# A two-block transformer on one Trainium2 core: the mixer's probabilities scaled by ScalarE, and its q and k norms split into two steps

## The chip, the core and the metric

The kernel runs on one core of a Trainium2 chip. The metric is the device time of one execution in microseconds; three runs are given, with their median. A profile of one execution gives a span (first to last instruction) and, for every instruction, when it started and how long it took. The engines are TensorE (PE; its weight loads, PEld, are listed apart), VectorE (DVE), ScalarE (ACT), GpSimd (POOL) and the DMA queues, which SyncE (SP) issues here.

## The reference

512 tokens of 1024 channels, float32. The first block has two layers: differential attention (8 heads, two softmaxes a head, their difference normalised per head), a gated FFN with a 3-wide convolution, a gated embedding; then the same with windowed attention. The second block is what most of the change is in, the *mixer*:

```python
h = rmsnorm(x, g_mix); proj = h @ w_in
a_in, q, k, v, f_logit, gate_a, gate_b = split(proj)
y_conv = silu(layernorm(causal_depthwise_conv(glu(a_in), w_dw, b_dw))) @ w_conv_out   # 31 taps, 512 channels
q, k = rmsnorm per head (8 heads of 64)
s = q k^T / 8 + c[q] - c[k], causal        # c: running sum of log sigmoid(f_logit + b_forget)
y_attn = softmax(s) v @ w_attn_out
x = x + (sigmoid(gate_a) * y_conv + sigmoid(gate_b) * y_attn) @ w_out
```

followed by a second gated FFN. All of it must come out in float32.

## The kernel before

Each float32 operand is held as a high and a low part, and a product is three matmuls: high with high, high with low, low with high (lines 188, 189, 190, in `mm3`). Weights arrive by DMA as `wr`; `wh` is cast from them by ACT (line 157) and `wl` is subtracted by DVE or POOL (line 158). `split` (lines 180 to 184) makes the two parts of an activation: ACT writes the high part, DVE the low one. All 512 tokens are one tile of 128 channels by 512 columns (the free dimension), so a projection (`dense`) is 24 matmuls of 512 columns.

The stages follow one another: differential attention from about 60 to 330 us of the span, FFN, embedding, windowed attention, FFN, embedding, the mixer from about 1340 to 1665, the last FFN.

**The order of the work.** The program is written as generators that yield where other work may step in. A scheduler then puts every engine's instructions in an order of its own, by place in the program and by what is ready in its model, and each engine runs its list strictly in that order. Tiles come from pools of a few buffers per tag. PSUM has 2 banks of tag `acc` (projections), 3 of `sc` (scores `ps_s` and sums of squares `ps_ss`), 1 of `po` and 2 of `tp`; they are handed out in program order. In SBUF the tag `C` of pool `fp` has 3 buffers, which the norm's `isq`, `isl`, `dg`, `iy` and POOL's convolution product `tap` share.

**The norm.** `inv_rms` (line 406) is used by both attentions. It takes the bank `ps_ss` first; with `eps` given (differential attention) `row_mm` puts two matmuls with diagonals `dg` (lines 211, 217) into it. Then ACT squares (`isq`, line 413) and copies (`ish`, 416), POOL or DVE subtracts (`isl`, 417), two matmuls add (lines 418, 419), ACT takes logarithm, exponential and a square, and DVE does two steps (424, 425) to `iy`. `head_norm` of the differential attention calls it on each head's output (POOL subtracts, DVE for heads 5 and 6). In the mixer `unit_heads` (line 968) reads a projection, calls `inv_rms` without `eps`, multiplies (972) and splits into `qhl`; `qk(m)` does so for k, yields, for q, yields, and then copies both by DMA into the stacks `st` of a pair of heads.

**The mixer's attention.** `head` (line 1000 on) has four row tiles of 128, 256, 384 and 512 columns: scores into an `sc` bank, DVE adds the decay and takes the maximum (1021), ACT exponentiates and sums (1026, recorded as line 146), DVE inverts the sum (1027) and scales (1028), PE transposes (1036), `split` makes `ah` and `al`, three matmuls add to `ps_o`. The first start is `qk(0)`, `vproj(0)`, `glu(2)`, `glu(3)` one after another (1056); the loop over heads (1064 to 1075) then mixes in the other projections, and after each row tile a convolution tap for POOL: `tap` times a weight (921) into a `C` buffer, added to `cacc` (924).

Of the kernel before, what the change touches and what calls it, by code (L numbers as in the profile page):

```python
# [19 lines left out]
P = 128  # L20
# [71 lines left out]
def build(tc, nc, a, out):  # L92
# [313 lines left out]
    def inv_rms(u, sel, n, eps=None, eng=G):  # L406


        ps = att.tile([P, T], F32, tag="sc", name="ps_ss", bufs=BANKS["sc"])
        if eps is not None:  # L410
            row_mm(ps, eps, eng, False)
        sq = fp.tile([P, T], F32, tag="C", name="isq")
# [3 lines left out]
        S.copy(out=sh, in_=sq)  # L416
        eng.tensor_tensor(out=sl, in0=sq, in1=rd(sh), op=ALU.subtract)
        TE.matmul(ps, sel, sh, start=eps is None, stop=False)
        TE.matmul(ps, sel, sl, start=False, stop=True)
# [5 lines left out]
        V.scalar_tensor_tensor(out=y, in0=sq, scalar=-3.0 * n / 64, in1=y, op0=ALU.add, op1=ALU.mult)  # L425
        return y, inv_rms_factor(n)


    def diff_attention(nm, nxt):
# [77 lines left out]
        def head_norm(hd):  # L507

            o = of[hd]
            eps = sm.tile([P, 4], F32, tag="eps", name="eps", bufs=2)  # L510
            s0 = sums[hd][:, :, 0]
            V.scalar_tensor_tensor(out=eps, in0=s0, scalar=P * EPS, in1=s0, op0=ALU.mult, op1=ALU.mult)
            eng = V if hd in HNV else G
            w, _ = inv_rms(o, onesr, P, eps, eng)
            eng.tensor_tensor(out=o, in0=o, in1=w, op=ALU.mult)
# [342 lines left out]
    def mix(nm, nxt):  # L858
# [109 lines left out]
        def unit_heads(ps, g, tag, bufs):  # L968

            u = evac_scaled(ps, nm.rb)  # L970
            w, f = inv_rms(u, blkr, 64, None, V)
            V.tensor_tensor(out=u, in0=u, in1=w, op=ALU.mult)
# [3 lines left out]
            split(hl[:, 0], hl[:, 1], u, gs)  # L976
            return hl

        sts = {}

        def qk(m):

            pk = dense("w_qk2", 2 * m + 1, x)
            hk = unit_heads(pk, gqk[:, 1:2], "hk", 1)
            yield
            pq = dense("w_qk2", 2 * m, x)
            hq = unit_heads(pq, gqk[:, 0:1], "hq", 1)
            yield
            for j in range(2):
                sl = slice(64 * j, 64 * j + 64)  # L990
# [11 lines left out]
        def head(hd):  # L1002
# [7 lines left out]
            for i in range(4):  # L1010
# [16 lines left out]
                V.reciprocal(out=su, in_=su)  # L1027
                V.tensor_scalar(out=e[:, :wd], in0=e[:, :wd], scalar1=su, scalar2=None, op0=ALU.mult)
                ee.append(e)
# [25 lines left out]

        for _ in chain(qk(0), vproj(0), *(glu(m) for m in (2, 3))):
            pass
        for m in (2, 3):
# [277 lines left out]
```

## Time and profile before

| | |
|---|---|
| runs | 2095.48, 2098.79, 2099.24 us; median 2098.79 |
| profiled execution | 2097.09 us, its span 2095.3 us |
| mean granted TensorE clock | 0.983 of 2.4 GHz |
| PE busy | 2013.4 us, 96% of the span |
| DVE / ACT / POOL busy | 1378.0 / 899.4 / 454.7 us |

PE's share says that it is nearly always at work, so that an engine beside it matters only where PE stands still. Where that is, the windows and the waits tell. 1.8 us of the execution lie outside the span.

### The profile page before, as it was taken

Reading aid. Unit: us, or ns where it says so; the run is one execution under the profiler, and the core shown is the slowest. Engines: PE = TensorE matmul, PEld = TensorE weight load, DVE = VectorE, ACT = ScalarE, POOL = GpSimd, SP = SyncE. Lnnn points to the kernel's source line nnn. Section 1 sums busy time; section 2 is a strip of 40 time slices with the busy share of each in tenths; the row PEclk is TensorE's granted clock in tenths of the full one; section 3 lists DMA queues with packets and bytes.
Section 4 is the critical chain, followed back from the end, with each engine's and each line's share of the span. In section 5 each row is a group of like instructions: output and inputs, shape, how many; then the busy total and the mean of one; then the engine's idle time right before and its main releaser. Section 6 shows DMA issues by size and latency. Waiting matters only on the chain.

```text
span 2095.3 us, 25046 instructions
## 1 busy us (share of the span) xinstructions
PE 2013.4 (96%) x9374; PEld 1655.5 (79%) x9374; DVE 1378.0 (66%) x2189; ACT 899.4 (43%) x1431; POOL 454.7 (22%) x322
## 2 busy tenths in 40 slices
PE   7999889999999999889999999999999899999999
PEld 6888668888888877668888888778778688888887
DVE  7776858747466757777647466778889764434443
ACT  5565635424244435554424235446546343222221
POOL 2464322000002226310000001305599030000000
PEclk9999989999999999999999999999999999999999
DMA  4543422233233253112232323233322232232232
GB/s 164 167 121 105 147 71 91 82 109 101 92 100 132 100 171 111 41 41 91 90 110 92 101 94 115 94 108 112 88 86 71 81 101 96 96 101 96 95 101 91
DMA packets 69465, 212.43 MB, mean 101 GB/s; under 512 B 9568, under 2 KB 9568, under 8 KB 68832
## 3 DMA queue, kind: packets, MB, share of 16 engines
q1 hardware_dynamic: 69344, 210.84, 31.5%
q8 instruction: 74, 1.21, 0.2%
q14 instruction: 47, 0.39, 0.1%
HBM read 179.31 MB, written 6.29 MB: 89 GB/s over the span
## 4 chain that ended last, share of the span: by engine, by line
PE 80%; DVE 9%; POOL 5%; issue 2%; ACT 2%; DMA 2%; SPq 1%; DVEq 0%; POOLq 0%; ACTq 0%
PE ps_d L188 25%; PE ps_d L190 24%; PE ps_d L189 24%; POOL cacc L924 3%; POOL tap L921 1%; DVE wl L158 1%; PE ps_o L189 1%; PE ps_s L395 1%; PE ps_o L188 1%; PE ps_o L190 1%; PE ps_s L396 1%; DMA qst<-rt 1%; SPq L385 1%; PE ps_t L674 1%; DVE xq L184 1%
## 5 line engine op out<-in xcount | busy, mean ns | idle before, releaser
L157 ACT CAST wh<-wr 128x1024 fp32r<-128x1024 f32 (+1 forms) x323 | 338.0, 1048 | 659.0 <-PE ps_d L189 551.2
L188 PE MATMUL ps_d<-xO,wh 128*128 128x512 f32 x1400 | 547.2, 392 | 5.6 <-ACT wh L157 3.2
L190 PE MATMUL ps_d<-xO,wl 128*128 128x512 f32 (+1 forms) x1400 | 547.2, 391 | 0.8 <-DVE wl L158 0.8
L189 PE MATMUL ps_d<-xV,wh 128*128 128x512 f32 (+1 forms) x1400 | 546.4, 391 | 0.0
L158 DVE TENSOR_TENSOR wl<-wr,wh 128x1024 fp32r<-128x1024 f32 x286 | 367.3, 1286 | 90.3 <-ACT wh L157 87.9
L188 PEld LDWEIGHTS ps_d<-xO,wh 128*128 128x128 f32 x1400 | 262.8, 188 | 62.5 <-ACT wh L157 4.5
L190 PEld LDWEIGHTS ps_d<-xO,wl 128*128 128x128 f32 (+1 forms) x1400 | 262.7, 188 | 57.5 <-DVE wl L158 2.0
L189 PEld LDWEIGHTS ps_d<-xV,wh 128*128 128x128 f32 (+1 forms) x1400 | 262.9, 188 | 55.6 <-DVE xV L184 0.2
L271 POOL TENSOR_TENSOR ss<-ss,sq 128x512 f32<-128x512 f32 x44 | 69.4, 1577 | 815.4 <-ACT sq L269 801.9
L314 DVE TENSOR_TENSOR u<-ps_d,rb 128x512 f32<-128x512 f32 x156 | 106.3, 687 | 203.5 <-PE ps_d L190 196.4
L189 PE MATMUL ps_d<-gl,wh 128*128 128x512 f32 x528 | 204.3, 389 | 0.0
L188 PE MATMUL ps_d<-gh,wh 128*128 128x512 f32 x528 | 203.0, 389 | 0.0
L190 PE MATMUL ps_d<-gh,wl 128*128 128x512 f32 x528 | 203.0, 389 | 0.0
L188 PE MATMUL ps_d<-xq,wh 128*128 128x512 f32 x448 | 179.3, 404 | 21.8 <-ACT wh L157 10.1
L190 PE MATMUL ps_d<-xq,wl 128*128 128x512 f32 x448 | 179.4, 401 | 1.3 <-DVE wl L158 1.3
L189 PE MATMUL ps_d<-xq,wh 128*128 128x512 f32 x448 | 180.0, 402 | 0.4 <-DVE xq L184 0.4
L763 DVE TENSOR_TENSOR h<-h,ps_d 128x512 f32<-128x512 f32 x72 | 48.6, 685 | 176.7 <-PE ps_d L190 176.7
L188 PEld LDWEIGHTS ps_d<-xq,wh 128*128 128x128 f32 x448 | 86.7, 194 | 41.9 <-ACT wh L157 10.3
L188 PEld LDWEIGHTS ps_d<-gh,wh 128*128 128x128 f32 x528 | 99.1, 188 | 20.6
L190 PEld LDWEIGHTS ps_d<-gh,wl 128*128 128x128 f32 x528 | 99.1, 188 | 20.6
L189 PEld LDWEIGHTS ps_d<-gl,wh 128*128 128x128 f32 x528 | 99.1, 188 | 20.5
L158 POOL TENSOR_TENSOR wl<-wr,wh 128x1024 fp32r<-128x1024 f32 x37 | 90.5, 2449 | 109.0 <-ACT wh L157 94.3
(313 smaller groups left out, 3112.2 us busy)
## 6 DMA issues: line engine op xcount, KB each, us to landing
wr<-w_up SPq DMA_DIRECT2D x132, 512.0 KB, 3.4
wr<-w_dn SPq DMA_DIRECT2D x66, 512.0 KB, 3.5
wr<-w_qk SPq DMA_DIRECT2D x34, 512.0 KB, 3.5
qst<-rt SPq DMA_DIRECT2D x64, 128.0 KB, 2.7
wr<-w_pg SPq DMA_DIRECT2D x16, 512.0 KB, 3.5
wr<-w_g SPq DMA_DIRECT2D x16, 512.0 KB, 3.4
wr<-w_v SPq DMA_DIRECT2D x14, 512.0 KB, 3.5
st<-qhl SPq DMA_DIRECT2D x48, 128.0 KB, 2.3
```

Source lines behind the costliest of these rows:

```text
L157: S.copy(out=hi, in_=raw)
L158: lo_eng[0].tensor_tensor(out=lo, in0=raw, in1=rd(hi), op=ALU.subtract)
L184: V.scalar_tensor_tensor(out=lo, in0=src, scalar=scale, in1=rd(hi), op0=ALU.mult, op1=ALU.subtract)
L188: TE.matmul(ps, lh, rh, start=start, stop=False)
L189: TE.matmul(ps, lh, rl, start=False, stop=False)
L190: TE.matmul(ps, ll, rh, start=False, stop=stop)
L271: (V if self.first and k not in SSP else G).tensor_tensor(out=self.ss, in0=self.ss, in1=sq, op=ALU.add)
L314: V.tensor_tensor(out=u, in0=ps, in1=rb, op=ALU.mult)
L385: Q.dma_start(out=rd(t[64 * b : 64 * b + 64]), in_=rd(hl[32 * j : 32 * j + 32, 2 * z : 2 * z + 2]))
L395: TE.matmul(ps, q[:, qc], k[:, kc], start=True, stop=False)
L763: V.tensor_tensor(out=h[m], in0=h[m], in1=ps, op=ALU.add)
L924: G.tensor_tensor(out=accs[m], in0=accs[m], in1=t, op=ALU.add)
```

## The change

The scaling of the probabilities (line 1028 before, 1033 after) is written for ACT: a copy with the inverted sum as its scale. `inv_rms` becomes a generator with two steps: squares and their two parts; then, after a `yield`, the bank, the matmuls and the rest. `unit_heads` and `qk` pass the break on, so in the mixer the second step of the norm of k comes after another projection, and the second step of q's after one more. At the start the program's order is now k's projection and first step, v's projection, rest of k's norm with q's projection and first step, half of `glu(2)`, rest of q's norm with the stacks, and what is left of the glus. `head_norm` runs both steps at once, but in it the bank and the two `dg` matmuls now come behind `isq`, `ish` and `isl`.

```diff
--- before.py
+++ after.py
@@ -406,15 +406,16 @@
     def inv_rms(u, sel, n, eps=None, eng=G):
 
 
-        ps = att.tile([P, T], F32, tag="sc", name="ps_ss", bufs=BANKS["sc"])
-        if eps is not None:
-            row_mm(ps, eps, eng, False)
         sq = fp.tile([P, T], F32, tag="C", name="isq")
         S.activation(out=sq, in_=u, func=AF.Square)
         sh = fp.tile([P, T], F32R, tag="A", name="ish")
         sl = fp.tile([P, T], F32R, tag="C", name="isl")
         S.copy(out=sh, in_=sq)
         eng.tensor_tensor(out=sl, in0=sq, in1=rd(sh), op=ALU.subtract)
+        yield
+        ps = att.tile([P, T], F32, tag="sc", name="ps_ss", bufs=BANKS["sc"])
+        if eps is not None:
+            row_mm(ps, eps, eng, False)
         TE.matmul(ps, sel, sh, start=eps is None, stop=False)
         TE.matmul(ps, sel, sl, start=False, stop=True)
         y = fp.tile([P, T], F32, tag="C", name="iy")
@@ -423,7 +424,7 @@
         S.activation(out=sq, in_=y, func=AF.Square, scale=0.125)
         V.scalar_tensor_tensor(out=sq, in0=ps, scalar=epsn[n] if eps is None else 0.0, in1=sq, op0=ALU.add, op1=ALU.mult)
         V.scalar_tensor_tensor(out=y, in0=sq, scalar=-3.0 * n / 64, in1=y, op0=ALU.add, op1=ALU.mult)
-        return y, inv_rms_factor(n)
+        yield y
 
 
     def diff_attention(nm, nxt):
@@ -511,7 +512,7 @@
             s0 = sums[hd][:, :, 0]
             V.scalar_tensor_tensor(out=eps, in0=s0, scalar=P * EPS, in1=s0, op0=ALU.mult, op1=ALU.mult)
             eng = V if hd in HNV else G
-            w, _ = inv_rms(o, onesr, P, eps, eng)
+            *_, w = inv_rms(o, onesr, P, eps, eng)
             eng.tensor_tensor(out=o, in0=o, in1=w, op=ALU.mult)
 
         ox = Quads()
@@ -968,24 +969,28 @@
         def unit_heads(ps, g, tag, bufs):
 
             u = evac_scaled(ps, nm.rb)
-            w, f = inv_rms(u, blkr, 64, None, V)
+            steps = inv_rms(u, blkr, 64, None, V)
+            yield next(steps)
+            w, f = next(steps), inv_rms_factor(64)
             V.tensor_tensor(out=u, in0=u, in1=w, op=ALU.mult)
             gs = sm.tile([P, 1], F32, tag="gs", name="gs")
             V.tensor_scalar(out=gs, in0=g, scalar1=f, scalar2=None, op0=ALU.mult)
             hl = ma.tile([P, 2, T], F32R, tag=tag, name="qhl", bufs=bufs)
             split(hl[:, 0], hl[:, 1], u, gs)
-            return hl
+            yield hl
 
         sts = {}
 
         def qk(m):
 
-            pk = dense("w_qk2", 2 * m + 1, x)
-            hk = unit_heads(pk, gqk[:, 1:2], "hk", 1)
-            yield
-            pq = dense("w_qk2", 2 * m, x)
-            hq = unit_heads(pq, gqk[:, 0:1], "hq", 1)
-            yield
+            uk = unit_heads(dense("w_qk2", 2 * m + 1, x), gqk[:, 1:2], "hk", 1)
+            next(uk)
+            yield
+            hk = next(uk)
+            uq = unit_heads(dense("w_qk2", 2 * m, x), gqk[:, 0:1], "hq", 1)
+            next(uq)
+            yield
+            hq = next(uq)
             for j in range(2):
                 sl = slice(64 * j, 64 * j + 64)
                 q, k, kl = (ma.tile([P, T], F32R, tag="st", name="st", bufs=9) for _ in range(3))
@@ -1025,7 +1030,7 @@
                 V.tensor_scalar(out=mx, in0=mx, scalar1=-1.0, scalar2=None, op0=ALU.mult)
                 act(out=e[:, :wd], in_=e[:, :wd], func=AF.Exp, bias=mx, scale=1.0, accum_out=su)
                 V.reciprocal(out=su, in_=su)
-                V.tensor_scalar(out=e[:, :wd], in0=e[:, :wd], scalar1=su, scalar2=None, op0=ALU.mult)
+                S.activation(out=e[:, :wd], in_=e[:, :wd], func=AF.Copy, scale=su)
                 ee.append(e)
                 yield
             po = att.tile([64, T], F32, tag="po", name="ps_o", bufs=1)
@@ -1053,8 +1058,9 @@
                 split(vt[t][0][:, cols], vt[t][1][:, cols], pss[t], nm.rt[:, t : t + 1])
             yield
 
-        for _ in chain(qk(0), vproj(0), *(glu(m) for m in (2, 3))):
-            pass
+        q0, g23 = qk(0), chain(glu(2), glu(3))
+        for g in (q0, vproj(0), q0, g23, q0, g23, g23, g23):
+            next(g)
         for m in (2, 3):
             glu_gate(m)
         wide(False)
```

The order on the engines differs in two stretches, the differential attention and the mixer; in the others it is the same. Three places:

**PE in the differential attention, the norm of the first head's output beside a later head's scores** (`ps_ss` with `dg`, `ish`, `isl` is the norm; `ps_s` with `kst` or `klo` are scores; `ps_t` transposes; `ps_d` with `wh`, `xq` a projection that fills in; the numbers tell the tiles apart, and `ps_s_948` is the same score tile in both). Before, a piece that begins 12 rows behind the norm's first matmul:

```order
L493 MATMUL ps_t_771<-cn_82,e_759 128x128 x4
L217 MATMUL ps_ss_904<-dg_911,onesr_84 128x512
L189 MATMUL ps_d_1027<-wl_1038,xq_141 128x256
L190 MATMUL ps_d_1027<-wh_1037,xq_142 128x256
L395 MATMUL ps_s_948<-kst_418,qst_428 128x512
L396 MATMUL ps_s_948<-klo_416,qst_428 128x512
L188 MATMUL ps_d_1028<-wh_1031,xq_107 128x256
L189 MATMUL ps_d_1028<-wl_1032,xq_107 128x256
```

Now, from the same norm's first matmul on:

```order
L217 MATMUL ps_ss_910<-dg_914,onesr_84 128x512
L395 MATMUL ps_s_948<-kst_418,qst_428 128x512
L396 MATMUL ps_s_948<-klo_416,qst_428 128x512
L395 MATMUL ps_s_954<-kst_423,qst_431 128x512
L396 MATMUL ps_s_954<-klo_417,qst_431 128x512
...
L217 MATMUL ps_ss_910<-dg_917,onesr_84 128x512
L419 MATMUL ps_ss_910<-ish_906,onesr_84 128x512
L420 MATMUL ps_ss_910<-isl_907,onesr_84 128x512
L396 MATMUL ps_s_992<-klo_416,qst_428 128x512
L395 MATMUL ps_s_998<-kst_423,qst_431 128x512
L396 MATMUL ps_s_998<-klo_417,qst_431 128x512
```

The norm's four matmuls now stand within 23 rows, before within 97; its first one has moved 122 rows later, and the score tile `ps_s_948`, which was handed out behind it, 107 rows later. The 136 rows ahead of the norm's first matmul now hold no score, and from its last one on 50 rows hold ten score tiles, transposes and products with v, and no projection.

**PE at the start of the mixer** (`ps_ss` with `blkr` is the norm of k or q of the first two heads). Before:

```order
L217 MATMUL ps_bc<-dg,onesr 128x512
L189 MATMUL ps_d<-xV,wh 128x512
L190 MATMUL ps_d<-xO,wl 128x512
L418 MATMUL ps_ss<-ish,blkr 128x512
L419 MATMUL ps_ss<-isl,blkr 128x512
L188 MATMUL ps_d<-xO,wh 128x512
L189 MATMUL ps_d<-xV,wh 128x512
L418 MATMUL ps_ss<-ish,blkr 128x512
```

Now:

```order
L188 MATMUL ps_d<-xO,wh 128x512
L189 MATMUL ps_d<-xV,wh 128x512
L419 MATMUL ps_ss<-ish,blkr 128x512
L188 MATMUL ps_d<-xO,wh 128x512
L189 MATMUL ps_d<-xV,wh 128x512
L190 MATMUL ps_d<-xO,wl 128x512
```

Both norms stood at the end of a projection, three rows from each other; now each stands inside a projection, with v's projection ahead of the first, and 61 rows between the two.

**POOL at the last norm of the mixer** (the rows with their waits). Before:

```order
L921 TENSOR_TENSOR tap<-pad,dwh 128x512 [waits DVE_49]
L924 TENSOR_TENSOR cacc<-cacc,tap 128x512 [waits Pool_49]
L921 TENSOR_TENSOR tap<-pad,dwh 128x512 [waits PE_49]
L924 TENSOR_TENSOR cacc<-cacc,tap 128x512 [waits Pool_49]
L921 TENSOR_TENSOR tap<-pad,dwh 128x512 [waits Pool_49]
```

Now:

```order
L922 TENSOR_TENSOR tap<-pad,dwh 128x512 [waits DVE_49,PE_49]
L925 TENSOR_TENSOR cacc<-cacc,tap 128x512 [waits Pool_49]
L922 TENSOR_TENSOR tap<-pad,dwh 128x512 [waits Pool_49]
L925 TENSOR_TENSOR cacc<-cacc,tap 128x512 [waits Pool_49]
L922 TENSOR_TENSOR tap<-pad,dwh 128x512 [waits PE_49]
```

The last tap that waits for PE (for a norm's `isl` to be read, so that its `C` buffer comes free) is two taps later than before; two taps and their additions fewer stand behind it. On PE the matmul that it waits for has moved 35 rows later.

## Rows read from the trace of the kernel before

**Rows 1.** The page, its first part: busy time of each engine, its share of the span, and the number of instructions.

```profile
PE 2013.4 (96%) x9374; PEld 1655.5 (79%) x9374; DVE 1378.0 (66%) x2189; ACT 899.4 (43%) x1431; POOL 454.7 (22%) x322
```

**Rows 2.** The windows view: for each stretch (us from the start of the span) its length, the busy time of PE, PEld, DVE, ACT and POOL with the number of instructions, the granted clock of TensorE as a share of 2.4 GHz, the DMA share and GB/s.

```profile
60.00:330.00 270.00, 248.67 (x1322) 208.86 (x1321) 200.58 (x337) 148.98 (x290) 117.96 (x67) 0.96 0.39 116
88.70:124.80 36.10, 35.55 (x227) 31.77 (x226) 26.49 (x52) 24.66 (x52) 17.63 (x10) 1.00 0.32 90
1340.00:1400.00 60.00, 54.16 (x284) 42.53 (x283) 49.97 (x95) 28.60 (x45) 15.86 (x15) 1.00 0.23 76
1400.00:1480.00 80.00, 78.10 (x421) 66.20 (x420) 65.86 (x129) 45.46 (x87) 30.98 (x23) 1.00 0.43 126
1480.00:1520.00 40.00, 35.74 (x169) 28.49 (x168) 34.76 (x69) 20.93 (x45) 27.13 (x21) 0.91 0.29 79
1520.00:1580.00 60.00, 55.28 (x273) 43.84 (x272) 50.68 (x102) 30.82 (x65) 56.38 (x43) 0.97 0.26 75
1580.00:1640.00 60.00, 56.97 (x249) 46.23 (x248) 56.42 (x71) 34.49 (x48) 42.99 (x29) 1.00 0.27 88
```

**Rows 3.** The waits view of the stretch 1340 to 1580: who waited for whom, us in total, times, the longest.

```profile
POOL tap L921 <- PE ps_ss L419: 91.5, 6, 58.8
...
PEld ps_o L189 <- DVE al L181: 4.1, 5, 2.5
...
PEld ps_t L1036 <- DVE e L1028: 3.3, 5, 1.2
```

**Rows 4.** The view of groups by line and shape, DVE, 1418 to 1552, line 1028: busy us and mean ns of one, then the idle time before them.

```profile
L1028 DVE TENSOR_SCALAR e<-e,su 128x384 f32<-128x384 f32 x8 | 9.0, 1128 | 0.2
L1028 DVE TENSOR_SCALAR e<-e,su 128x512 f32<-128x512 f32 x8 | 7.8, 971 | 0.1
L1028 DVE TENSOR_SCALAR e<-e,su 128x256 f32<-128x256 f32 x8 | 7.4, 926 | 0.2
...
L1028 DVE TENSOR_SCALAR e<-e,su 128x128 f32<-128x128 f32 x8 | 4.9, 618 | 0.2
```

**Rows 5.** The timeline of DVE, 1462 to 1472: start us, us, instruction.

```profile
1464.20 1.24 DVE L1028 TENSOR_SCALAR e<-e,su 128x128 f32<-128x128 f32 x1
...
1465.51 0.35 DVE L1028 TENSOR_SCALAR e<-e,su 128x256 f32<-128x256 f32 x1
...
1471.50 0.42 DVE L1028 TENSOR_SCALAR e<-e,su 128x384 f32<-128x384 f32 x1
```

**Rows 6.** The timeline of POOL in the same stretch, its last long row there.

```profile
1464.01 1.30 POOL L924 TENSOR_TENSOR cacc<-cacc,tap 128x512 f32<-128x512 f32 x1
```

**Rows 7.** The view of groups by line and shape, ACT, 1380 to 1560: the exponentials of the mixer's scores, by width.

```profile
L146 ACT ACTIVATE e<-e,mx 128x512 f32<-128x512 f32 x8 | 5.7, 718 | 8.7 <-DVE mx L1025 8.6
...
L146 ACT ACTIVATE e<-e,mx 128x384 f32<-128x384 f32 x8 | 4.9, 607 | 0.0
...
L146 ACT ACTIVATE e<-e,mx 128x256 f32<-128x256 f32 x8 | 4.0, 503 | 0.1
...
L146 ACT ACTIVATE e<-e,mx 128x128 f32<-128x128 f32 x8 | 3.2, 399 | 2.7 <-DVE mx L1025 2.7
```

**Rows 8.** The timeline of PE at the start of the mixer; in brackets the idle time before the row and what ended it.

```profile
1383.16 0.50 PE L188 MATMUL ps_d<-xO,wh 128*128 128x512 f32 x1 [0.76 <-ACT wh L157]
...
1385.30 0.50 PE L418 MATMUL ps_ss<-ish,blkr 128*128 128x512 f32 x1 [1.40 <-ACT ish L416]
```

**Rows 9.** The timeline of PE in the mixer's attention: three of its longer waits.

```profile
1461.41 0.30 PE L395 MATMUL ps_s<-st 128*128 128x128 f32 x1 [1.42 <-issue]
...
1494.56 0.48 PE L189 MATMUL ps_o<-al,xq 128*64 128x256 f32 x1 [2.34 <-DVE al L181]
...
1541.64 0.44 PE L1036 MATMUL ps_t<-cn,e 128*128 128x128 f32 x2 [0.97 <-DVE e L1028]
```

**Rows 10.** The timeline of PE at the last norm of the mixer (that of q of the last head pair) and some 35 matmuls on.

```profile
1520.79 0.39 PE L419 MATMUL ps_ss<-isl,blkr 128*128 128x512 f32 x1
...
1528.05 0.39 PE L189 MATMUL ps_d<-xV,wh 128*128 128x512 f32 x1
1528.27 0.39 PE L190 MATMUL ps_d<-xO,wl 128*128 128x512 f32 x1
```

**Rows 11.** The timeline of POOL: the last wait for a norm, the start of the long unbroken run, and that run's end.

```profile
1521.26 1.04 POOL L921 TENSOR_TENSOR tap<-pad,dwh 128x512 f32<-128x512 f32 x1 [3.59 <-PE ps_ss L419]
...
1526.81 1.95 POOL L921 TENSOR_TENSOR tap<-pad,dwh 128x512 f32<-128x512 f32 x1 [0.63 <-DVE iy L425]
...
1609.94 15.01 POOL L924 TENSOR_TENSOR cacc<-cacc,tap 128x512 f32<-128x512 f32 x9
```

**Rows 12.** The view of groups by line and shape, DVE, 88 to 300 (the differential attention): the three large operations of its softmax.

```profile
L483 DVE TENSOR_REDUCE nmx<-ps_s 128x1 f32<-128x512 f32 x53 | 35.6, 682 | 12.3 <-PE ps_s L396 12.1
L490 DVE SCALAR_TENSOR_TENSOR e<-e,rec 128x512 f32<-128x512 f32 x29 | 28.0, 967 | 0.3
L181 DVE TENSOR_TENSOR at<-ps_t,at 128x512 fp32r<-128x512 f32 x29 | 19.8, 683 | 4.8 <-ACT at L180 4.6
```

**Rows 13.** The timeline of PE in the differential attention: the first and the last matmul of the first head norm's ps_ss, and the longest wait.

```profile
89.50 0.40 PE L217 MATMUL ps_ss<-dg,onesr 128*128 128x512 f32 x1
...
103.44 0.40 PE L419 MATMUL ps_ss<-isl,onesr 128*128 128x512 f32 x1
...
279.19 0.80 PE L188 MATMUL ps_d<-xq,wh 128*128 128x512 f32 x1 [5.12 <-DVE h L526]
```

## The prediction

> **What bounds the kernel now.** I read the page's busy shares first: PE has 2013.4 us of work [rows 1], so time can only be won where it stands still, or where its clock falls. The windows [rows 2] say where that is in the two stretches that the change reorders. In the differential attention (60 to 330) PE is busy for 248.67 of 270 us, so it idles 21.3; at the start of the mixer (1340 to 1400) it idles 5.8, and in the mixer's attention (1400 to 1580) 180 − 169.12 = 10.9. The granted clock is 0.91 in 1480 to 1520, which is some 7 us at 1.2 instead of 2.4 GHz and costs 3.6; it falls in the stretch where PE's share is lowest.
>
> Beside PE, DVE is the full engine of the mixer's attention: 65.86 + 34.76 + 50.68 = 151.3 of 180 us, 84%. ACT has 97.2, 54%. Then comes POOL: 56.38 of 60 us from 1520 on [rows 2], one unbroken run from 1526.81 to 1609.94 + 15.01 = 1624.95 [rows 11], behind which the convolution is closed. So three things end this part together: PE, DVE's softmax, and POOL's taps, which cannot start sooner than the last norm lets go of a buffer.
>
> **The scaling: DVE minus 29.2, ACT plus 17.8 us.** On DVE the 32 scalings take 9.0 + 7.8 + 7.4 + 4.9 = 29.1 us [rows 4]. ACT has none of them; the nearest rows are the exponentials of the same tiles, same widths, an operand per partition: 8 x (0.718 + 0.607 + 0.503 + 0.399) = 17.8 us [rows 7]. Without their maximum's bias they may be a little shorter, so 17.8 is the upper end and the value I take; ACT goes to 115 of 180 us (64%), DVE to 122 (68%). Both lie beside PE. What PE gets is what it waited for: 3.3 us in weight loads for `e` from line 1028 and 4.1 for `al` [rows 3], which DVE makes late when a scaling stands ahead of it, as at 1494.56 (2.34) and 1541.64 (0.97) [rows 9].
>
> Why it is so dear on DVE shows in one place: 128 columns took 1.24 us at 1464.20, while POOL ran an addition from 1464.01 to 1465.31; 256 and 384 columns took 0.35 and 0.42 with POOL idle [rows 5, 6]. So the scaling pays mostly for POOL being busy, and ACT's rows do not show that.
>
> The Trainium skill speaks against this edit: "ScalarE: Activation LUTs", section "Rules for kernel authors", sends multiplications to VectorE. With POOL idle the trace agrees (0.42 against 0.607 us for 384 columns), and by the rule alone the edit would cost engine time; the sum of the group, 29.1 against 17.8, goes the other way.
>
> New is a hop: ACT now waits for DVE's reciprocal, with weight casts and the next exponentials behind it in its list. At most places another exponential stands between, so I set this at nothing; if that cover is gone, it is a rival below.
>
> **The two-step norm at the start of the mixer: −4 us.** Two waits vanish, 0.76 for `wh` and 1.40 for `ish` [rows 8], since now a projection runs through both norms. The others of the 5.8 us (the row broadcast, the first weights) partly stay: I take 4, bounds 2 and 5.8.
>
> **The mixer's attention: −2 us more, because POOL caps it.** Of 10.9 us of idle time and 3.6 of clock, 6.2 + 3.6 = 9.8 lie before 1520 [rows 2]. I take half, 5 us, as gone: the waits for `e` and `al` go, those for the stacks (1.42 at 1461.41 [rows 9]) do not. So PE is X = 4 + 5 = 9 us early at the last norm; bounds 2 and 15.6. But that norm now stands 35 rows later, where PE is at 1528.27 instead of 1520.79 [rows 10], and up to 1.5 us more, since the rows ahead of it aren't the same. POOL's last wait ends with it. From 1521.26 to 1624.95 POOL worked 103.7 us; two taps with their additions less stand behind the wait now, 4.7 us, so 99. POOL ends at 1528.8 − X + 99 = about 1628 − X, against 1625: the mixer gains X − 3 = **6 us**, bounds −1 (a loss of 1) and 12. The last two heads' scores also have fewer rows between norm and stacks, so PE may wait 2 to 5 us for the DMA there; POOL's run covers it.
>
> **The differential attention: +5 us.** This is a side effect. The bank `ps_ss` is now asked for behind `isq`, `ish` and `isl`, and banks of a tag go out in program order, so the scores behind it wait too: `ps_s_948` moves 107 rows back, and then ten score tiles stand together without a projection between. They are five row tiles. For each, DVE does two maxima, a combination and a low part: 2 x 0.682 + 0.967 + 0.683 = 3.0 us [rows 12], 15 us for five. PE's work there is 20 score matmuls and some 7 of the norms at 0.22 (start to start in [rows 10]), 24 half-wide ones at half of it, 16 transposes at a quarter: 5.9 + 2.6 + 0.9 = 9.4 us. So PE idles 5 to 6 more where from 88.70 to 124.80 it idled 0.55 [rows 2], and with the two `dg` behind one another rather 7. Of the later norms I put 3 on the second pair, −2 on the third (before, its bank was held through the whole norm, as from 89.50 to 103.44 in [rows 13], and that ends now), and −3 on the end, where the wait of 5.12 at 279.19 [rows 13] finds more fillers left over. Sum +5; bounds −4 (the freed bank wins everywhere) and +15 (7, 5 and 3 in three pairs, nothing back).
>
> **Sum.** −4 −2 + 5 = −1 us on the profiled execution of 2097.09, so 2096; the median of the runs is 1.7 above that execution. I give **2097**, between the two bases. A measurement of this kernel can tell about 0.2%, 4.2 us.
>
> **The rivals.**
> *A, slower: bunched scores.* The place is the differential attention, the price is DVE's 3.0 us a row tile against 1.9 of PE. It decides if fillers no longer stand between scores in more than the first pair: 7 + 5 + 3 − 3 = +12, and with X = 7 a mixer of −4: +8, 2105. For it speak the order and DVE's load there, 200.58 of 270 [rows 2]; against it, that this leaves DVE slack between the pairs. PE idling longer also brings the clock down, as it is in [rows 2] for that stretch (0.96).
> *B, faster: DVE was the bound.* The differential attention comes out even (the bank that is free for 14 us of each norm pays for the first pair), +1, and with DVE at 68% nearly all waits in the mixer go, X = 12, −9: −8, 2089. For it speak 84% of DVE and the inflated scalings; against it POOL's cap, which leaves 3 us of every gain. The Trainium skill, "SBUF — State Buffer", section "Who interferes with whom", has DVE and POOL share one port pair under an exclusive lock; the 1.24 us beside POOL's addition agree. By it POOL's run would shorten as well.
> *C, no change: the mixer's gain is lost.* Stacks and POOL's last wait come as late as before (X = 3, gain 0), the differential attention +1: 2098.
> *D, slower: ACT in order.* A scaling that waits for DVE holds the cast of the weights behind it, PE waits for `wh`; with 32 scalings and 0.2 us each 6.4 us lost in the mixer: mixer 0, +5, 2102.
>
> **How the numbers follow.** Forecast 0.34 (its own range 2091 to 2102), A 0.23, B 0.31, C 0.07, D 0.05. Faster by over 0.2%: B, and 0.05 of the forecast's range, 0.36. Within: the rest of the forecast but 0.02, and C, 0.34. Slower: A, D, 0.02, 0.30. For 8 in 10 the range must reach into A and B past their centres: 2084 to 2109.
>
> **What would show it.** Scalings on ACT at 0.40 to 0.72 us, 17 to 18 us in sum; DVE under 125 us between 1400 and 1580; no wait for `ish` at the start of the mixer; POOL's long run ending 4 to 8 us sooner relative to the mixer's start; PE in the first 36 us behind 88.7 with 6 to 9 us of idle time, and the differential attention ending 5 us later. I am wrong if that stretch ends sooner or over 10 later, or if PE, not POOL, is last at the end of the convolution.

## The result, and the profile after

The changed kernel took 2116.95 us (median of four runs, 2116.09 to 2120.22) against 2097.14 of the kernel before (four runs, 2093.43 to 2099.24): ratio 1.0097, 95% interval 1.0086 to 1.0109. It is slower by about 20 us, outside the range. The profiled execution took 2117.41 us, its span is 2115.6, its mean granted clock 0.977 (0.983 before). The page's first line answers to [rows 1]:

```profile
PE 2023.7 (96%) x9374; PEld 1662.8 (79%) x9374; DVE 1361.0 (64%) x2157; ACT 911.2 (43%) x1463; POOL 453.9 (21%) x322
```

DVE lost 17.0 us of work, ACT gained 11.8, PE shows 10.3 more at a lower clock: no engine has 20 us more to do. The windows answer to [rows 2]. The mixer now starts 17.5 us later, so its windows are moved by that; the second window begins 27.9 us behind the stage's first score, as 88.70 did before:

```profile
60.00:330.00 270.00, 239.31 (x1254) 197.40 (x1253) 190.29 (x327) 141.00 (x280) 106.52 (x62) 0.95 0.37 114
88.00:124.10 36.10, 31.04 (x186) 26.71 (x185) 18.71 (x39) 18.57 (x39) 14.04 (x8) 0.97 0.34 102
1357.50:1417.50 60.00, 57.15 (x295) 46.44 (x294) 48.63 (x87) 27.47 (x44) 15.88 (x15) 0.97 0.26 89
1417.50:1497.50 80.00, 76.33 (x406) 65.05 (x406) 60.14 (x119) 47.91 (x94) 30.65 (x21) 0.98 0.38 113
1497.50:1537.50 40.00, 37.49 (x187) 29.83 (x186) 31.42 (x73) 28.49 (x62) 31.20 (x24) 0.96 0.32 93
1537.50:1597.50 60.00, 51.21 (x228) 39.43 (x227) 37.74 (x77) 30.54 (x66) 52.81 (x42) 0.83 0.24 70
1597.50:1657.50 60.00, 60.00 (x266) 49.72 (x265) 58.32 (x75) 36.76 (x54) 43.32 (x29) 1.00 0.26 88
```

In 60 to 330 PE is busy for 9.4 us less and idles 30.7 instead of 21.3; the first 36 us alone hold 5.1 us of idle time, before 0.55. In the mixer's first two windows PE idles less than before at the start (2.85 for 5.84), then more (3.67 for 1.90); in the fourth it idles 8.8, before 4.7, and the clock is 0.83, before 0.97.

Stage by stage: the differential attention, from its first score to the first matmul of the stage behind it, took 269.1 us, before 254.2 (**+14.9**); the windowed attention, from its first matmul to its last score, 170.2, before 166.8 (+3.4), with the same order of instructions; the mixer, from a point 434.5 us behind the last score of the windowed attention (1340.0 before, 1357.5 now), reached the end of its convolution (PE's first `ps_cs`, the sum over the channels) at 302.5, before 299.1 (**+3.4**). The rest of the span is 1.4 us shorter.

**Differential attention.** The timeline of PE around the first head norm, which answers to [rows 13]:

```profile
107.61 0.40 PE L217 MATMUL ps_ss<-dg,onesr 128*128 128x512 f32 x1
...
112.65 0.40 PE L420 MATMUL ps_ss<-isl,onesr 128*128 128x512 f32 x1
...
115.12 0.50 PE L395 MATMUL ps_s<-kst,qst 128*128 128x512 f32 x1 [0.95 <-ACT e L146]
...
116.80 0.50 PE L395 MATMUL ps_s<-kst,qst 128*128 128x512 f32 x1 [0.94 <-ACT e L146]
...
120.96 0.63 PE L494 MATMUL ps_t<-cn,e 128*128 128x128 f32 x4 [2.04 <-DVE e L491]
122.53 1.09 PE L494 MATMUL ps_t<-cn,e 128*128 128x128 f32 x4 [0.94 <-DVE e L491]
```

From its first to its last matmul the norm now takes some 5 us, where [rows 13] had 14, but it begins 18 us later; behind it PE waits for ACT's exponentials and DVE's combinations, one row tile after another. From 110 to 130 PE is busy for 13.1 us of 20, DVE for 13.4 and ACT for 11.6: none of them is full, each waits for another's piece of a row tile. The waits of PE over 60 to 330 (us in total, times, longest):

```profile
PE ps_s L395 <- ACT e L146: 11.7, 8, 3.4
...
PE ps_t L494 <- DVE e L491: 4.5, 3, 2.0
```

The first line, scores that wait until ACT has read a bank of `sc`, was 5.6 us before, the second 2.0.

**The mixer.** ACT's scalings, 1400 to 1600, against [rows 4, 7]:

```profile
L1033 ACT ACTIVATE e<-e,su 128x512 f32<-128x512 f32 x8 | 5.8, 720 | 0.0
...
L1033 ACT ACTIVATE e<-e,su 128x384 f32<-128x384 f32 x8 | 4.9, 608 | 0.7 <-DVE su L1032 0.7
...
L1033 ACT ACTIVATE e<-e,su 128x256 f32<-128x256 f32 x8 | 4.0, 502 | 0.0
...
L1033 ACT ACTIVATE e<-e,su 128x128 f32<-128x128 f32 x8 | 3.1, 391 | 0.1
```

17.8 us, as forecast. DVE worked 60.14 + 31.42 + 37.74 = 129.3 us in the 180 from 1417.5 on, ACT 106.9. Waits of the whole mixer (1340 to 1665) in the changed kernel:

```profile
ACT ish L413 <- DVE qhl L184: 10.3, 4, 4.0
...
PE ps_d L188 <- DVE pad L888: 3.7, 1, 3.7
...
PE ps_t L1041 <- ACT e L1033: 2.8, 2, 1.8
```

The first stood in the kernel before too, but for less than half of this:

```profile
ACT ish L416 <- DVE qhl L184: 4.3, 3, 3.0
```

The wait for `pad` is new. In the third ACT stands where DVE stood, with 1.9 us in three waits before. Three timelines of one place show what the first two are, DVE, ACT and PE in turn:

```profile
1476.28 1.52 DVE L184 SCALAR_TENSOR_TENSOR qhl<-u,gs,qhl 128x512 fp32r<-128x512 f32 x1
...
1478.61 0.87 DVE L414 TENSOR_TENSOR isl<-isq,ish 128x512 fp32r<-128x512 f32 x1 [0.62 <-ACT ish L413]
1479.40 0.68 DVE L888 TENSOR_TENSOR pad<-ps_d,rb 128x512 f32<-128x512 f32 x1
```

```profile
1474.79 0.61 ACT L410 ACTIVATE isq<-u 128x512 f32<-128x512 f32 x1
1477.89 0.62 ACT L413 CAST ish<-isq 128x512 fp32r<-128x512 f32 x1 [2.49 <-DVE qhl L184]
```

```profile
1475.87 0.60 PE L1041 MATMUL ps_t<-cn,e 128*128 128x128 f32 x4
1480.13 0.64 PE L188 MATMUL ps_d<-xO,wh 128*128 128x512 f32 x1 [3.67 <-DVE pad L888]
```

ACT has `isq` at 1475.4, and then stands 2.49 us until DVE has written `qhl`: `ish` gets the buffer of tag A (three buffers in the same pool, which `u` and `ish` share) that the norm of k held for `u`. DVE's `isl` stands behind `ish`, `pad` behind `isl`, and PE's projection waits 3.67 us for `pad`. Both norms are now in flight at once, each holding its buffers through a projection.

The last norm, against [rows 10], and the two waits behind it:

```profile
1543.48 0.39 PE L420 MATMUL ps_ss<-isl,blkr 128*128 128x512 f32 x1
...
1547.98 1.06 PE L1041 MATMUL ps_t<-cn,e 128*128 128x128 f32 x3 [1.79 <-ACT e L1033]
...
1553.68 0.69 PE L189 MATMUL ps_o<-al,xq 128*64 128x512 f32 x1 [1.77 <-DVE al L181]
```

1543.48 is 186.0 us from the mixer's start; before it was 180.8. From 1548.6 on 17 us of this place run at a clock of 0.50, with 12.97 us of PE work in them, so some 6.5 us are lost to the clock. And the taps of DVE, before and after (timeline of DVE, first and last row of `pacc`):

```profile
1573.68 1.51 DVE L912 TENSOR_SCALAR pacc<-pad,dwh,sp 128x512 f32<-128x512 f32 x2
...
1635.62 0.75 DVE L915 SCALAR_TENSOR_TENSOR cacc<-pad,dwh,pacc 128x512 f32<-128x512 f32 x1
```

```profile
1597.30 1.52 DVE L913 TENSOR_SCALAR pacc<-pad,dwh,sp 128x512 f32<-128x512 f32 x2
...
1655.23 0.75 DVE L916 SCALAR_TENSOR_TENSOR cacc<-pad,dwh,pacc 128x512 f32<-128x512 f32 x1
```

DVE's taps start 23.6 us later, 6.1 more than the shift of the mixer; the program puts `pacc` into banks of the attention's tags, and the attention's last `ps_o` moved by 7.2. POOL's run behind the last norm took 98.65 us (forecast 99), 3.39 of them a wait for a tap that ACT makes, and ended at 1642.6. Before, this is what followed on POOL's end, first on DVE, then on PE:

```profile
1624.98 0.69 DVE L1105 TENSOR_TENSOR cacc<-pacc,cacc 128x512 f32<-128x512 f32 x1 [0.51 <-POOL cacc L924]
```

```profile
1639.06 0.50 PE L1111 MATMUL ps_cs<-csh,onesr 128*128 128x512 f32 x1 [2.81 <-ACT csh L180]
```

And now on DVE:

```profile
1642.65 0.69 DVE L1111 TENSOR_TENSOR cacc<-pacc,cacc 128x512 f32<-128x512 f32 x1 [0.70 <-POOL cacc L925]
```

DVE waits for POOL's sum in the midst of its own last taps. Before, PE then waited 2.81 us for the sum of all channels; in the changed kernel PE comes to `ps_cs` at 1660.0 without a wait: PE itself is last there.

### The profile page after: what moved, and what is told of

Read it like the earlier page. It is cut to its first block, busy times and chain, and to the rows that moved or that the text cites. A ratio compares the mean times of both kernels' runs of the same rounds, so it can differ in the third digit from the quotient of the medians.

```text
span 2115.6 us, 25040 instructions
## 1 busy us (share of the span) xinstructions
PE 2023.7 (96%) x9374; PEld 1662.8 (79%) x9374; DVE 1361.0 (64%) x2157; ACT 911.2 (43%) x1463; POOL 453.9 (21%) x322
## 4 chain that ended last, share of the span: by engine, by line
PE 82%; DVE 9%; ACT 3%; issue 3%; DMA 1%; SPq 1%; POOL 1%; DVEq 0%; ACTq 0%; POOLq 0%
PE ps_d L188 26%; PE ps_d L190 25%; PE ps_d L189 25%; DVE wl L158 1%; PE ps_s L395 1%; PE ps_o L189 1%; PE ps_o L188 1%; ACT e L146 1%; PE ps_o L190 1%; PE ps_s L396 1%; DVE e L650 1%; SPq L385 1%; DVE e L491 1%; PE ps_t L675 1%; ACT wh L157 1%
## 5 line engine op out<-in xcount | busy, mean ns | idle before, releaser
L188 PE MATMUL ps_d<-xq,wh 128*128 128x512 f32 x448 | 177.5, 401 | 15.7 <-ACT wh L157 8.7
L189 PE MATMUL ps_d<-xq,wh 128*128 128x512 f32 x448 | 177.4, 396 | 1.2 <-DVE xq L184 1.2
```

Of the source, the lines that this page charges most:

```text
L188: TE.matmul(ps, lh, rh, start=start, stop=False)
L189: TE.matmul(ps, lh, rl, start=False, stop=False)
```

## Experiments

Stage times from the profile of each, in us; the last three columns count from the mixer's start. One profile stands for each kernel; the windowed attention, whose order of instructions is the same in all, spreads over 4.4 us, so a few us in one cell can be the clock.

| run | differential att. | windowed att. | last norm | last `ps_o` | end of conv. |
|---|---|---|---|---|---|
| before | 254.2 | 166.8 | 180.8 | 227.9 | 299.1 |
| after | 269.1 | 170.2 | 186.0 | 235.1 | 302.5 |
| e1_scale | 253.7 | 170.2 | 173.8 | 221.9 | 291.7 |
| e2_diff | 269.9 | 166.2 | 180.9 | 228.4 | 299.2 |
| e3_twostep | 252.3 | 166.1 | 185.5 | 232.5 | 299.8 |
| e4_mixer_all | 252.4 | 168.7 | 185.9 | 238.9 | 306.4 |
| t2_dg_early | 244.2 | 168.3 | 181.7 | 228.0 | 299.9 |
| t4_bank_tp | 245.9 | 165.9 | 180.7 | 228.1 | 299.0 |
| e5_start_only | 252.2 | 166.6 | 179.0 | 224.2 | 293.9 |
| e6_later_only | 254.7 | 170.2 | 181.7 | 226.7 | 294.7 |
| e9_hl_two | 253.5 | 169.0 | 173.5 | 222.6 | 293.5 |
| e10_hl_one | 253.5 | 170.3 | 175.9 | 221.6 | 291.5 |
| e11_ish_hl | 253.9 | 170.3 | 187.0 | 232.0 | 300.1 |
| e12_isl_hl | 252.2 | 167.1 | 191.8 | 234.0 | 303.5 |
| b1_scale_dg | 241.0 | 167.1 | 176.1 | 225.6 | 294.0 |
| b2_scale_tp | 245.8 | 169.6 | 173.5 | 221.4 | 291.3 |
| b3_scale_dg_hl | 241.2 | 167.1 | 176.4 | 224.5 | 292.0 |

**The parts apart.** First the scaling alone, in the kernel before (e1_scale):

```diff
-                V.tensor_scalar(out=e[:, :wd], in0=e[:, :wd], scalar1=su, scalar2=None, op0=ALU.mult)
+                S.activation(out=e[:, :wd], in_=e[:, :wd], func=AF.Copy, scale=su)
```

> Only the scaling goes to ScalarE; norms as before. Theory (the hop to ScalarE costs little, DVE's relief is real): 17.8 us on ACT, 29 us less on DVE in the mixer, the last two heads no later than before, 2 to 6 us faster than the kernel before. Rival (in-order ScalarE makes the last two heads late, the 10 us that the changed kernel loses there): 4 to 10 us slower, with PE waiting for e from the scaling behind the last norm.

2089.93 us against 2097.85, ratio 0.9963 (0.9949 to 0.9976): 7.9 us faster. The waits of the mixer and the windows of its attention:

```profile
PEld ps_o L189 <- DVE al L181: 1.5, 4, 0.6
...
PEld ps_t L1036 <- ACT e L1028: 0.2, 1, 0.2
```

```profile
1401.80:1481.80 80.00, 80.00 (x437) 68.47 (x436) 58.82 (x121) 53.48 (x101) 34.78 (x26) 1.00 0.43 126
1481.80:1521.80 40.00, 37.85 (x190) 30.65 (x189) 30.17 (x73) 28.28 (x62) 30.16 (x23) 0.96 0.34 93
1521.80:1581.80 60.00, 55.56 (x265) 44.60 (x264) 42.22 (x81) 35.38 (x70) 58.12 (x44) 0.94 0.26 75
```

The waits for `al` fell from 4.1 to 1.5, those for `e` from 3.3 to 0.2; in the first 80 us PE does not idle. The last norm comes 7.0 us sooner, the end of the convolution 7.4: what PE wins is kept.

Only the norm of the differential attention's heads as in the change (`inv_rms2` is the change's `inv_rms`; all else as before; e2_diff):

```diff
-            w, _ = inv_rms(o, onesr, P, eps, eng)
+            *_, w = inv_rms2(o, onesr, P, eps, eng)
```

> Only the differential attention's norm gets the new order (bank and the dg matmuls behind isl); mixer as before. Theory (bunched scores): 14 to 18 us slower, nearly the whole loss of the change, all of it between 60 and 330 us of the span but for up to 3 us of clock behind it. Rival (the mixer is what costs): under 6 us slower.

2117.45 against 2097.85, ratio 1.0088 (1.0071 to 1.0106). By the medians nearly the whole loss is here: 19.6 of 19.8 us. The profile is of a run at 2112.22, the second shortest of six (clock 0.981; the four longer ones have 0.978 to 0.980); its span is 15.1 us longer than before. Its differential attention takes 269.9 us, 15.7 more; what the longer runs lose besides stands in no profile.

```profile
60.00:330.00 270.00, 241.67 (x1250) 198.21 (x1249) 189.44 (x324) 139.17 (x277) 104.97 (x60) 0.93 0.38 114
```

Only the two steps in the mixer and its start (e3_twostep): the change, with two lines taken back.

```diff
-            *_, w = inv_rms(o, onesr, P, eps, eng)
+            w, _ = inv_rms1(o, onesr, P, eps, eng)
...
-                S.activation(out=e[:, :wd], in_=e[:, :wd], func=AF.Copy, scale=su)
+                V.tensor_scalar(out=e[:, :wd], in0=e[:, :wd], scalar1=su, scalar2=None, op0=ALU.mult)
```

> Only the mixer's norms in two steps; scaling on DVE, differential attention as before. Theory (a later last norm bunches the last two heads): start of the mixer 4 us shorter, the last heads 6 to 10 us longer, in sum 0 to 5 us slower. Rival (the two steps win, the scaling on ScalarE costs): 3 to 6 us faster.

2097.54 against 2097.85, ratio 1.0002 (0.9991 to 1.0012): nothing. The shorter start is given back before the last norm, which is 4.7 us late; the wait of `ish` for `qhl` is here too, so it does not come from the scaling:

```profile
ACT ish L435 <- DVE qhl L184: 11.7, 4, 4.0
...
PE ps_t L1063 <- DVE e L1055: 3.7, 3, 2.5
```

Everything in the mixer, the norm of the heads as before (e4_mixer_all; the first of the two lines above alone):

> The whole change but with the differential attention's norm as before. Theory (parts add): 15 to 18 us of the 20 go away, so 2 to 5 us slower than the kernel before. Rival (the mixer gains once the stages ahead are undisturbed): 2 to 6 us faster.

2098.11 against 2097.85, ratio 1.0009 (0.9994 to 1.0023). The 7.9 us of the scaling are gone when the two steps stand beside it. The runs fall in two groups, 2092.16 to 2099.80 with clocks of 0.979 to 0.983 and 2103.25 to 2105.66 with 0.977 to 0.978; the profile is of the slower one, and shows half clock behind the last norm, as after:

```profile
1520.00:1570.00 50.00, 43.09 (x176) 32.97 (x175) 27.48 (x65) 24.84 (x57) 46.52 (x36) 0.76 0.25 67
```

**The norm of the differential attention.** Two things differ from before there: the bank of tag `sc` is asked for late, and its first matmul waits for a `dg` that is made late. t2_dg_early is e2_diff with both `dg` built ahead of `isq`, in tag A (`row_dg` is the first half of `row_mm`):

```diff
+        dgs = row_dg(eps, eng)
         sq = fp.tile([P, T], F32, tag="C", name="isq")
...
-        if eps is not None:
-            row_mm(ps, eps, eng, False)
+        for z in range(2):
+            TE.matmul(ps, onesr, dgs[z].rearrange("p a b -> p (a b)"), start=z == 0, stop=False)
```

> The differential attention's norm as in the change, but with its two diagonals dg built ahead of the squares (in the buffers of tag A), so that the bank's first matmul is ready early again; mixer as before. Theory (the scores queue behind a bank whose first matmul is late): scores and projections alternate again and the 19 us of the run with the new norm alone go away: within 4 us of the kernel before. Rival (the loss comes from the norm's own chain, squares ahead of everything): 10 to 19 us slower.

2088.78 against 2097.17, ratio 0.9956 (0.9943 to 0.9968): not only is the loss undone, it is faster than the kernel before. t4_bank_tp is e2_diff with the late `dg`, but the bank from the tag of the transposes:

```diff
-        ps = att.tile([P, T], F32, tag="sc", name="ps_ss", bufs=BANKS["sc"])
+        ps = att.tile([P, T], F32, tag="tp", name="ps_ss")
```

> The differential attention's norm as in the change, diagonals late, but its bank from the tag tp of the transposes, not from the three banks of the scores; mixer as before. Theory (scores queue behind that bank): most of the 19 us go, 0 to 8 us slower. Rival (the diagonals come late on POOL and the norm's chain itself is longer): still 14 to 20 us slower.

2089.87, ratio 0.9965 (0.9952 to 0.9979). The windows 60 to 330 of the two, and a wait of PE in each, t2_dg_early first:

```profile
60.00:330.00 270.00, 254.82 (x1360) 214.09 (x1359) 205.62 (x354) 151.60 (x292) 117.04 (x67) 0.97 0.40 121
```

```profile
PE ps_d L188 <- DVE h L566: 1.1, 1, 1.1
```

```profile
60.00:330.00 270.00, 252.72 (x1355) 211.93 (x1354) 203.52 (x354) 149.27 (x292) 115.90 (x67) 0.98 0.40 120
```

```profile
PE ps_ss L217 <- POOL dg L211: 0.5, 1, 0.5
```

The bank's tag alone, with `dg` as late as before and still in tag C, brings the stage from 269.9 to 245.9 us: what costs most is that scores stand in one queue behind that bank for the three banks of `sc`, while the wait for the late `dg` itself is 0.5 us in t4_bank_tp. With the bank out of that queue, or with its first matmul ready at once, the stage is 8 to 10 us shorter than before. The two are not alike on the way. Where 60 us of matmul work are done, behind the first pair of heads, t2_dg_early is 2 us behind the kernel before, t4_bank_tp still 7, and the changed kernel 10.7; so the other bank does not undo the loss of the first pair, and the early `dg` does. (t2_dg_early also takes both `dg` out of tag C; no run has them early in C.) The win lies late: beyond 160 us of matmul work PE loses some 18 us before, some 5 in t2_dg_early, some 8 in t4_bank_tp (time lost is the time beyond the sum of the matmuls' undisturbed start-to-start distances; by how these are taken the figures move by 1 to 2 us), and the wait for `h`, 5.12 in [rows 13], is 1.1 in the former. That this win comes from banks that are no longer held for 14 us, as in [rows 13], is argued; no run parts it from the new order.

**The two steps in the mixer.** Scaling on ACT, two steps for the first head pair only (e5_start_only), and for the later ones only, with the start as before (e6_later_only, `m > 0`):

```diff
-            yield
+            if m == 0:
+                yield
             hk = next(uk)
+            if not (m == 0):
+                yield
```

> Scaling on ScalarE; two-step norms only for the first head pair (the start of the mixer), the later pairs in one step; differential attention as before. Theory (the two steps win at the start, and cost where the last norm comes late): 9 to 13 us faster than the kernel before, 2 to 5 faster than the scaling alone. Rival (the start gives nothing in the end, since the end of the attention sets the time): 6 to 9 us faster, as the scaling alone.

> Scaling on ScalarE; two-step norms only for the later three head pairs, the start in one step as before; differential attention as before. Theory (late norms bunch the last heads and the clock falls there): 0 to 4 us slower than the kernel before, 8 to 12 slower than the scaling alone. Rival (the loss sits at the start): 6 to 9 us faster, as the scaling alone.

2091.95 and 2093.82 against 2097.17, ratios 0.9975 (0.9967 to 0.9984) and 0.9985 (0.9976 to 0.9993). Neither reaches the scaling alone (0.9963), and neither of the numbers expected for either run came: against its gain of 7.9 the two steps lose 2.7 us in the first pair, where the intervals overlap, and 4.6 in the later ones; together 7.3 of the 8.2 that e4_mixer_all lost. Next the buffers: both mixer changes, with `ish` and `isl` written into the tile that `qhl` will take anyway, so that tags A and C are asked for less (e9_hl_two), and the same with the norm in one step and the start as before (e10_hl_one):

```diff
+            hl = ma.tile([P, 2, T], F32R, tag=tag, name="qhl", bufs=bufs)
...
-        sh = fp.tile([P, T], F32R, tag="A", name="ish")
-        sl = fp.tile([P, T], F32R, tag="C", name="isl")
+        sh, sl = hl[:, 0], hl[:, 1]
```

> Both mixer changes (scaling on ScalarE, norms in two steps), differential attention as before, but ish and isl of the mixer's norms are written into the tile qhl that their result goes to later, so they take no buffer of the tags A and C. Theory (u and ish of k, held through q's projection, use up the three buffers of A; ish then waits for qhl, isl and pad behind it, and PE for the bank of pad): the wait of PE for pad (3.7 us in the changed kernel) and those of ish for qhl (10.3 us) go, the long stretch of half clock at the last heads too, 6 to 12 us faster than the kernel before. Rival (the last norm is late because of its place in the program): 0 to 2 us from the kernel before, as with both mixer changes in A and C.

> Scaling on ScalarE, norms in one step, differential attention as before; ish and isl of the mixer's norms in qhl as in the run above. Control for it: theory (buffers matter only where u and ish live through a projection): within 4 us of the scaling alone, so 4 to 12 us faster than the kernel before. Rival (the buffers are what bounds the mixer in any order, POOL's taps above all): 12 to 18 us faster.

2090.54 and 2087.77 against 2096.82, ratios 0.9969 (0.9958 to 0.998) and 0.9958 (0.9946 to 0.997). With `ish` and `isl` out of the tags A and C the two-step norm keeps most of the scaling's gain: PE no longer waits for `pad`, nor `ish` for a buffer of tag A, the last norm is at 173.5 instead of 185.9 in e4_mixer_all, and in e9_hl_two these stretches run at full clock:

```profile
1481.30:1521.30 40.00, 40.00 (x214) 33.28 (x213) 32.76 (x75) 29.24 (x64) 35.29 (x26) 1.00 0.36 100
1521.30:1581.30 60.00, 55.54 (x277) 44.13 (x276) 43.01 (x86) 37.80 (x77) 58.04 (x44) 1.00 0.28 83
```

Of the waits for `e` this is left:

```profile
PE ps_t L1066 <- ACT e L1058: 0.2, 1, 0.2
```

Which tag was short? Only `ish` in that tile (e11_ish_hl, tag A relieved; its edit is shown), only `isl` (e12_isl_hl, tag C relieved):

```diff
-            sh, sl = hl[:, 0], hl[:, 1]
+            sh = hl[:, 0]
+            sl = fp.tile([P, T], F32R, tag="C", name="isl")
```

> Both mixer changes, differential attention as before; only ish is written into qhl, isl stays in tag C. Theory (tag A is what runs short: ish waits for u's buffer): as with both tiles in qhl, 5 to 8 us faster than the kernel before, no wait of ish for qhl. Rival (tag C, where isl, iy, isq and POOL's taps queue): as with neither, within 3 us of the kernel before.

> Both mixer changes, differential attention as before; only isl is written into qhl, ish stays in tag A. Theory (tag A runs short): as with neither, within 3 us of the kernel before. Rival (tag C): 5 to 8 us faster.

2098.49 and 2101.01 against 2096.99, ratios 1.0006 (0.9995 to 1.0017) and 1.0019 (1.0009 to 1.003). Neither alone helps, and e12_isl_hl is 4 us slower: both single-tag theories fell. With `ish` moved PE's wait for `pad` is gone, yet the last norm comes at 187.0; now there is a wait for a buffer of tag C, where the next `isq` waits for POOL's sum:

```profile
ACT isq L432 <- POOL cacc L951: 4.1, 1, 4.1
```

ACT also waits there for the DMA that reads the tile into the stacks, 11.6 us in sum; e9_hl_two has this wait too, with 12.6 us, and its last norm at 173.5, so it does not explain the difference between the two.

**The parts that pay, together.** The scaling with t2_dg_early's norm (b1_scale_dg), with t4_bank_tp's (b2_scale_tp), and the first with e10_hl_one's tile as well (b3_scale_dg_hl); the edits are those shown above.

> Scaling on ScalarE, and the differential attention's norm with its diagonals built first in the buffers of A; mixer's norms in one step. Theory (the two gains lie in different stages and add): 8 + 8, 13 to 18 us faster than the kernel before. Rival (they do not add): 6 to 10 us faster.

> Scaling on ScalarE, and the differential attention's norm with late diagonals and its bank from the tag tp; mixer's norms in one step. Theory (gains add): 13 to 18 us faster than the kernel before. Rival: 6 to 10 us faster.

> Scaling on ScalarE, the differential attention's norm with its diagonals built first in tag A, the mixer's norms in one step with ish and isl in qhl. Theory (in one step the mixer's buffers cost little): within 3 us of the same without the last part, 15 to 20 us faster than the kernel before. Rival: over 20 us faster.

2079.48 and 2083.75 against 2096.82, ratios 0.9915 (0.9902 to 0.9928) and 0.9938 (0.9927 to 0.995); 2076.88 against 2096.99, 0.9903 (0.9886 to 0.992). In b1_scale_dg the gains add: it has 17.3 us, its two parts 7.9 and 8.4. b2_scale_tp has 13.1, its parts 7.9 and 7.3. The third is 20.1 us faster than the kernel before, and 2.6 faster than the first, with intervals that overlap.

## Why the prediction was wrong

The sum was −4 −2 + 5 = −1. In the profiles the mixer came to +3.4, the differential attention to +14.9, the windowed attention to +3.4, and the rest to −1.4: +20.3. By the medians of the runs that change one place alone, the norm of the differential attention is worth 19.6 us and the mixer 0.3.

**The scaling: right.** 17.8 us on ACT, as taken from the exponentials. The Trainium skill, "ScalarE: Activation LUTs", "Rules for kernel authors", sends multiplications to VectorE; here the measurement decides against it, by 7.9 us. That POOL's work would shrink beside a relieved DVE, which rival B expected, did not come: 457.0 us in e1_scale, before 454.7. DVE came to 129.3 us, not 122, ACT to 106.9, not 115, in the whole change. Rival D, PE waiting for weights behind ACT's scalings, did not occur.

**The start of the mixer: right, if smaller.** At equal work PE was 2.5 us ahead behind the start, where 4 was forecast with bounds of 2 and 5.8; the wait for `ish` there is gone. Of the 5.7 us it was ahead further on, a part is the scaling's: e1_scale, with the start as before, is 2.7 ahead at that place.

**The differential attention: the place and the bunching right, the term mis-sized.** This is the step that failed and that decides: the term of +5 us measured +14.9, at the end of its bounds. By time lost at equal work, the first pair of heads cost 10.7 (forecast 7), the second 5 (3), the third gave 3.6 (2), and the end cost some 3 where it was to give 3. The count took DVE's 3.0 us a row tile for the limit and left out that a tile goes through ACT's exponential and back to DVE, in order: PE waits at 115.12 to 122.53 for one or the other, while DVE has 13.4 us of work in 20. And of the fillers left over at the end only the half came true: the wait for `h` fell from 5.12 to 0.6, that of 5.2 for `xq` stayed, and other places lost more. Rival A named this place, with 12 us for it; e2_diff has it alone.

**The mixer's attention: "X = 9 us early at the last norm" failed.** It was 5.2 late. The waits removed were right, as e1_scale shows, where the norm comes 7.0 early. What was put at nothing without a reason is that a norm cut in two holds `u`, `isq`, `ish` and `isl` through a projection, in the tags A and C with three buffers each. At one place it cost 6 us at equal work, in the last two heads 10, some 6.5 of it clock. e9_hl_two against e4_mixer_all shows the buffers of `ish` and `isl` as the cause, and e11_ish_hl and e12_isl_hl that both tags are short; the path by which tag C delays the last norm is read from waits and not shown by a run.

**"POOL caps it": failed.** That the formula for POOL's run held to 0.4 us is partly luck: the 98.65 us have a wait of 3.39 for ACT in them, where the forecast counted work alone. And POOL does not set the end. In the changed kernel PE comes last to the convolution's sum, without a wait, which the prediction had named as a sign of being wrong. In the kernel before PE did wait there, but 2.81 us, and between POOL's end at 1624.95 [rows 11] and that matmul lay ten taps of DVE, the last at 1635.62. In all seventeen profiles DVE waits 0.3 to 0.7 us for POOL's last sum; between the last `ps_o` and the end of the convolution PE has 295 or 296 matmuls and idles 0 to 3.9 us. So that time is 67.3 to 71.9 us, while the last `ps_o` itself ranges over 17.5: a gain or a loss in the attention passes through nearly whole. What POOL would take of a gain of PE alone no run shows, since in e1_scale POOL's end came sooner too, by 7.5 us.

**Not in the sum:** 3.4 us in the windowed attention, where nothing was changed: 23.9 us at a clock of 0.50 there, before 17.1. That is not the change's doing: the other profiles spread as far, as the last section shows.

**Open.** Why the two steps with their own tile are 3 us behind one step (e9_hl_two, e10_hl_one; their ranges overlap). A wait of ACT for the stacks' DMA to have read the tile, 12.6 us in the former's mixer, is a candidate that was not tried. Open is also why the runs of e4_mixer_all fall in two groups.

## What to carry to other kernels

Where buffers or banks are handed out in program order, moving a request is moving everyone behind it: ask late only for what can be filled at once, or take it from another queue, and see then who waits in that one. Cutting a step in two lengthens the life of every tile that crosses the cut; count them against the pool before counting the wait that goes. And before an engine is called the cap of a stage, look at the wait that ends the stage, at who is waited for, and at how long it is.

## What the runs showed of the hardware

The granted clock differs between profiles of one order of instructions: in the windowed attention, the same in all seventeen, 10.2 to 23.9 us ran at a clock of 0.50 (1.2 GHz), and the stage took 165.9 to 170.3 us.

In e4_mixer_all the same program made two groups of runs some 8 us apart. In the profile, of the slower one, the clock was 0.50 from 1533.1 to 1557.0, with 18.9 us of PE work in that time, so some 9.5 us are lost to it (an estimate: half of that work). PE had waited 1.79 us, to 1532.48, just before the clock fell, and three waits of 0.46 to 1.77 us followed while it was low. In the changed kernel it fell at 1548.6, again behind a wait of 1.79 us, to 1547.98. e9_hl_two has not these waits, though others of up to 1.42 us, and kept 1.00 there. So in these two profiles the clock costs more than the waits beside it; that it is what parts the two groups of runs fits their mean clocks, but no run of the faster group was profiled.
